# Attention with unnormalised probabilities: the denominators of two heads inverted together and applied to the output by GpSimd

## The chip, the cores and the metric

The kernel runs on one core of a Trainium2 chip. A core has a matrix engine (TensorE, PE in the profile, with its weight loads listed apart as PEld), a vector engine (VectorE, DVE), a scalar engine (ScalarE, ACT), GpSimd (POOL) and SyncE (SP), which issues most of the DMAs. The engines run their own instruction streams in order and wait for each other by semaphores. The metric is the device time of one execution in microseconds, the median of three runs.

## The reference

One layer of a hybrid encoder block over 1024 tokens of width 1024. What matters here is the neighbourhood attention: 16 heads of width 64 over a 16 x 64 grid of tokens, each query looking at a window of 8 x 16 keys, with a learned bias.

```python
s = jnp.einsum("bjhd,bajchd->bhjac", q_i, k_win).astype(jnp.float32) + bias.astype(jnp.float32)[None]
p = jax.nn.softmax(s.reshape(bsz, NA_HEADS, GRID_W, kh * NA_COLS), axis=-1)
p = p.reshape(bsz, NA_HEADS, GRID_W, kh, NA_COLS).astype(v.dtype)
return jnp.einsum("bhjac,bajchd->bjhd", p, v_win)
...
x = x + jnp.concatenate([y_ssm, y_na.astype(y_ssm.dtype)], axis=-1) @ w_out
```

The attention output and the output of a state-space mixer are put side by side and multiplied by `w_out`; a squared-ReLU MLP follows.

## The kernel before

The program is one stream of work written in a tile framework. The framework's scheduler plans the whole program with a simulated timeline and fixes the order of the instructions on each engine; on the chip each engine keeps that order. Products that need more than one pass are made from operands that are split in a high and a low part (`split_from_psum`, `split_na`, `load_w`: ScalarE writes the high part, VectorE or GpSimd the low part), three matmuls for each product.

The stages in order: input projection and state-space mixer, the projections of q, k and v, the attention stage, the end of the output projection, the MLP in two phases. The change lies in the attention stage (lines 773 to 1006).

**The heads.** Eight pairs of heads are worked through (line 983). `load_qkv(p)` loads q, k (high and low part) and v of a pair with SP's DMAs into tiles of two alternating pools; `bias_for(h)` loads the bias of one head (`braw`) and GpSimd adds a mask to it in three instructions (`mb`, L881, two buffers). `attend` then makes one head, `hh` being 0 or 1 in the pair, in eight blocks of 128 queries. A block `b` sees two or three blocks of 128 keys, so its scores are 128 x 256 or 128 x 384. Its steps are:

- two matmuls (L931, L934) write the scores into a PSUM tile `psc` (two buffers);
- VectorE adds the bias and finds the row's negated maximum (L939, with a second small instruction that reads the accumulator); ScalarE takes the exponential and its row sum `db` (L949, again with an accumulator read);
- VectorE inverts the row sum (L957) and multiplies the probabilities by it (L958);
- TensorE transposes the two or three 128 x 128 pieces (L962) into a PSUM tile `ptp` (two buffers, shared with `pty` below), ScalarE and VectorE split them into `pth` and `ptl` (L184, L185);
- `weigh(b - 3)` multiplies the values by the transposed probabilities of an earlier block (L908), and where four blocks of queries are complete ScalarE copies the high half and VectorE adds the low half into `yT` (L918, L919).

`yT` holds a pair's output as 128 rows (two heads of 64) by 1024 tokens in one buffer; after the pair SP stores it to `na_dr[p]` (L996).

**The filler.** Between the blocks the output projection is worked off: `w_out_part(0..2)` is a generator of 48 steps, each one an output tile of 12 matmuls of 128x512 (`po`, L178 to L180) and one VectorE addition (L833). Two steps are made ahead of the attention, then 44 over its 128 blocks (line 973), two behind the last block, and `fill(-1)` makes whatever is left. Parts 0 and 1 read the mixer's output from `y_dr`; part 2 reads `na_dr[0..3]`. Their weights come by `load_w`, which loads 512 KB, lets ScalarE write the high part (L148) and GpSimd the low part (L149).

**The end of the stage.** The fourth part of the output projection takes `na_dr[4..6]`, read back and split by ScalarE and GpSimd while pair 7 is worked on (lines 985 to 991), and the last pair's `yT`, split straight from SBUF by ScalarE (L789) and VectorE (L790). Its matmuls run in the loop at line 1069, with the products of `na_dr[4]`, `[5]`, `[6]` and of pair 7 as `k` = 0, 1, 2, 3 of each tile.

Of the kernel before, what the change touches and what calls it, by code (L numbers as in the profile page):

```python
# [1 line left out]

# [1 line left out]

# [14 lines left out]
P = 128  # L19
# [36 lines left out]
def hymba_block(  # L56
# [66 lines left out]
    y1_dr = dr.tile([NT, P, D], F32, name="y1_dr")  # L123
    y_dr = dr.tile([NT, P, D], F32, name="y_dr")
    na_dr = dr.tile([NT, P, D], F32, name="na_dr")
    cum_dr = dr.tile([2, P, P], F32, name="cum_dr")
    t2_dr = dr.tile([16, 16, 8, 384], F32, name="t2_dr")
    t1_dr = dr.tile([16, 8, 31, 24], F32, name="t1_dr")
# [644 lines left out]
    with ExitStack() as ph:  # L773
# [18 lines left out]
        def w_out_part(part, yt):  # L792
            for f in range(4 * part + len(yt), 4 * part + 4):
                yl = yp.tile([P, T], F32R, tag="yl", name="yl", bufs=4)
                yh = yp.tile([P, T], F32R, tag="yh", name="yh", bufs=4)
                yf = yl.bitcast(F32)
                if f < 8:
                    nc.sync.dma_start(
                        yf.rearrange("p (c f) -> p c f", c=NT),
                        y_dr[:, :, f * P : (f + 1) * P].rearrange("c p f -> p c f"),  # L800
                    )
                    pts = []
                    for h in range(2):
                        pt = ps_tp("pty")
                        for j in range(4):
                            c = 4 * h + j
                            nc.tensor.transpose(
                                pt[:, j * P : (j + 1) * P], yf[:, c * P : (c + 1) * P], ident
                            )
                        pts.append(pt)  # L810
                    for h in range(2):
                        s = slice(h * 512, (h + 1) * 512)
                        split_from_psum(
                            yh[:, s], yl[:, s], pts[h], pcol[:, 72 + f : 73 + f]
                        )
                else:
                    nc.sync.dma_start(yf, na_dr[f - 8])
                    split_na(yh, yl, yf, nc.gpsimd)
                yt.append((yh, yl))
            for h, t in ((h, t) for h in range(2) for t in range(NT)):  # L820
                if t == 0:
                    get = load_w_nat(w_out[0], 512 * part, 4, 512 * h, nc.gpsimd)
                pt = ps_mm("po")
                s = slice(t * P, (t + 1) * P)
                for k in range(4):
                    yh, yl = yt[k]
                    mm3(pt, yh[:, s], yl[:, s], *get(k), k == 0, k == 3)
                d = x2[:, t, h * 512 : (h + 1) * 512]
                if part == 0:
                    nc.sync.dma_start(  # L830
                        d, x[0, t * P : (t + 1) * P, h * 512 : (h + 1) * 512]
                    )
                nc.vector.tensor_tensor(d, d, pt, op=add)  # L833
                yield
# [54 lines left out]
        pth = ap.tile([P, NT, 3, P], F32R, name="pth", bufs=1)  # L889
        ptl = ap.tile([P, NT, 3, P], F32R, name="ptl", bufs=1)  # L890

        def attend(hh, mb, q, k, kl, v, yT):
            hp = slice(HD * hh, HD * hh + HD)
            nmx = ap.tile([P, 8], F32, tag="nmx", name="nmx")
            den = ap.tile([P, 8], F32, tag="den", name="den")
            pv = [ps_v("pv0"), None]

            def weigh(g):
                b0, b1 = max(g - 1, 0), min(g + 2, NT)
                for i in range(2):  # L900
                    c0, c1 = max(b0, 4 * i), min(b1, 4 * i + 4)
                    if c0 >= c1:
                        continue
                    first, last = g == 3 * i, g == 4 + 3 * i
                    if first and i:
                        pv[1] = ps_v("pv1")
                    for pt in (pth, ptl):
                        pvm = nc.tensor.matmul(  # L908
                            pv[i][:, (c0 - 4 * i) * P : (c1 - 4 * i) * P],
                            lhsT=v[:, g, hh],  # L910
                            rhs=pt[:, g, c0 - g + 1 : c1 - g + 1, :],
                            start=first and pt is pth,
                            stop=last and pt is ptl,
                            skip_group_check=True,
                        )
                    if last:
                        yo = to_grid(yT[hp], i)
                        nc.scalar.copy(yo, from_blocks(pv[i][0:HD]))  # L918
                        nc.vector.tensor_tensor(  # L919
                            yo, yo, from_blocks(pv[i][HD:P]), op=add  # L920
                        )
                return pvm

            for b in range(NT):
                g0, g1 = max(b - 1, 0), min(b + 2, NT)
                m = g1 - g0
                n = m * P
                o = (3 if b == 0 else 5 if b == NT - 1 else 0) * P
                qs, ks = slice(b * P, (b + 1) * P), slice(g0 * P, g1 * P)
                pt = ps_s("psc")  # L930
                nc.tensor.matmul(  # L931
                    pt[:, 0:n], lhsT=q[:, hh, qs], rhs=k[:, hh, ks], start=True, stop=False
                )
                mark = nc.tensor.matmul(  # L934
                    pt[:, 0:n], lhsT=q[:, hh, qs], rhs=kl[:, hh, ks], start=False, stop=True
                )
                pr = ap.tile([P, 384], F32, tag="pr", name="pr", bufs=4)
                db = den[:, b : b + 1]
                nc.vector.tensor_tensor_reduce(  # L939
                    pr[:, 0:n],  # L940
                    pt[:, 0:n],
                    mb[:, o : o + n],
                    scale=-1.0,
                    scalar=3.0e38,
                    op0=add,
                    op1=ALU.min,
                    accum_out=nmx[:, b : b + 1],
                )
                nc.scalar.activation(  # L949
                    pr[:, 0:n],  # L950
                    pr[:, 0:n],
                    AF.Exp,
                    bias=nmx[:, b : b + 1],
                    scale=-1.0,
                    accum_out=db,
                )
                nc.vector.reciprocal(db, db)  # L957
                nc.vector.tensor_scalar(pr[:, 0:n], pr[:, 0:n], db, None, op0=mul)  # L958
                pp = ps_tp("ptp")
                for j in range(m):  # L960
                    s = slice(j * P, (j + 1) * P)
                    nc.tensor.transpose(pp[:, s], pr[:, s], ident)  # L962
                s0 = 2 * g0 + b + 1
                hi, lo = (
                    t.rearrange("p g s q -> p (g s) q")[:, s0 : s0 + 2 * m - 1 : 2, :]
                    for t in (pth, ptl)
                )
                pv3 = pp[:, 0:n].rearrange("p (j q) -> p j q", q=P)
                split_from_psum(hi, lo, pv3)
                if b > 2:  # L970
                    weigh(b - 3)
                done[0] += 1
                if done[0] * 44 // 128 > (done[0] - 1) * 44 // 128:
                    with tc.issue_after(mark.ins):
                        fill()
            weigh(NT - 3)
            weigh(NT - 2)
            return mark, weigh(NT - 1)

        filler += [w_out_part(0, []), w_out_part(1, []), w_out_part(2, [])]  # L980
        last = []
        fill(2)
        for p in range(8):
            q, k, kl, v = load_qkv(p)
            if p == 7:
                for j, tag in enumerate(("q", "k", "v")):
                    hl = b0.tile([P, 2, T], F32R, tag=tag, name="hl", bufs=1)
                    yf = hl[:, 1].bitcast(F32)
                    nc.sync.dma_start(yf, na_dr[4 + j])
                    split_na(hl[:, 0], hl[:, 1], yf, nc.gpsimd)  # L990
                    last.append((hl[:, 0], hl[:, 1]))
            yT = yt.tile([P, T], F32, tag="yT", name="yT", bufs=1)
            for hh in range(2):
                marks = attend(hh, bias_for(2 * p + hh), q, k, kl, v, yT)
            if p < 7:
                nc.sync.dma_start(na_dr[p], yT)  # L996
            else:
                hl = b0.tile([P, 2, T], F32R, tag="kl", name="hl", bufs=1)
                split_na(hl[:, 0], hl[:, 1], yT, nc.vector)
                last.append((hl[:, 0], hl[:, 1]))  # L1000
        for i in (0, 1):
            with tc.issue_after(marks[i].ins):
                fill()
# [391 lines left out]
```

## Time and profile before

| | |
|---|---|
| median of three runs | 1681.8 us (1676.36 to 1685.55) |
| the profiled execution: span | 1676.4 us, equal to the fastest of the three runs to 0.1 us |
| its mean granted TensorE clock | 0.986 |
| attention stage, first softmax to last output tile | 674 to 966 us of the span |
| before it: projections and mixer | 0 to 674 us |
| behind it: end of the output projection | 966 to 1025 us |
| MLP | 1025 to 1676 us |

The busy time of TensorE in the profile counts overlapping matmuls once, and the end of each matmul is modelled, so a high busy share does not mean that no more matmuls would fit; the starts of matmuls that follow each other show how fast they are really issued. The list of waits names for each idle time of an engine the instruction that ended it.

### The profile page before, as it was taken

What the parts mean: (1) busy time and instruction counts of PE and PEld (TensorE: products, weight loads), DVE (VectorE), ACT (ScalarE), POOL (GpSimd) and SP (SyncE); (2) the same over time, 40 slices, a digit from 0 to 9 for tenths busy, and PEclk for the clock granted to TensorE, in tenths of its full rate; (3) what the DMA queues carried; (4) which work ended last, traced back from release to release, by engine and by line L of the source; (5) the groups of instructions that cost most, each with busy time, mean ns of one, the idle gap of its engine ahead of it and who ended that gap; (6) DMA issues with size and microseconds to landing.
All of it is one profiled execution on the core that took longest, in us unless ns stands there. A gap on an engine that the chain in (4) does not pass through costs nothing. (4 is left out here: it accounts for less than half of the span.)

```text
span 1676.4 us, 20931 instructions
## 1 busy us (share of the span) xinstructions
PE 1590.8 (95%) x7453; PEld 1297.3 (77%) x7453; DVE 1106.0 (66%) x1686; ACT 721.3 (43%) x1187; POOL 708.4 (42%) x506
## 2 busy tenths in 40 slices
PE   6999999998988899998999989999999989999999
PEld 5788888777766678887778767788888868888887
DVE  5767214788796852888898867544243387887863
ACT  5434223434343442556565533554444444433330
POOL 4000003888687862322243232244444465455551
PEclk9999999999999999999999999999999989999999
DMA  8113337876666785956664141353344386644231
GB/s 217 51 38 105 93 100 212 215 194 196 229 220 173 218 263 190 281 165 185 180 190 118 62 164 50 101 201 126 138 164 150 127 295 231 216 149 151 101 101 75
DMA packets 178755, 269.75 MB, mean 161 GB/s; under 512 B 14219, under 2 KB 105307, under 8 KB 178651
## 3 DMA queue, kind: packets, MB, share of 16 engines
q1 hardware_dynamic: 134667, 227.51, 44.1%
q10 hardware_dynamic: 42976, 37.23, 7.3%
q0 software_dynamic: 1008, 3.67, 0.5%
q8 instruction: 59, 0.97, 0.3%
q14 instruction: 45, 0.37, 0.1%
HBM read 185.21 MB, written 86.50 MB: 162 GB/s over the span
## 5 line engine op out<-in xcount | busy, mean ns | idle before, releaser
L760 POOL TENSOR_TENSOR wl<-wraw,wh 128x1024 fp32r<-128x1024 f32 x110 | 298.5, 2724 | 318.4 <-ACT wh L759 297.1
L759 ACT ACTIVATE wh<-wraw 128x1024 fp32r<-128x1024 f32 x110 | 115.6, 1054 | 149.7 <-PE px L745 50.8
L745 PE MATMUL px<-wh,ahl 128*128 128x512 f32 x512 | 162.5, 395 | 3.3 <-ACT ahl L759 3.3
L179 PE MATMUL pq<-wl,hTh 128*128 128x512 f32 x384 | 153.6, 402 | 4.9 <-DVE wl L149 4.8
L178 PE MATMUL pq<-wh,hTh 128*128 128x512 f32 x384 | 154.4, 405 | 3.5 <-ACT wh L148 3.5
L745 PE MATMUL px<-h,wh 128*128 128x512 f32 x496 | 156.0, 396 | 1.4 <-DVE x L1078 1.4
L180 PE MATMUL pq<-wh,hTl 128*128 128x512 f32 x384 | 152.9, 399 | 0.0
L760 DVE TENSOR_TENSOR ahl<-ar,ahl 128x1024 fp32r<-128x1024 f32 x56 | 115.1, 2062 | 23.2 <-ACT ahl L759 22.1
L759 ACT ACTIVATE ahl<-ar 128x1024 fp32r<-128x1024 f32 x56 | 58.2, 1052 | 140.1 <-PE px L745 75.3
L745 PEld LDWEIGHTS px<-wh,ahl 128*128 128x128 f32 x512 | 97.0, 190 | 25.0 <-ACT ahl L759 3.7
L745 PEld LDWEIGHTS px<-h,wh 128*128 128x128 f32 x496 | 93.2, 188 | 24.0 <-ACT h L184 1.6
L149 DVE TENSOR_TENSOR wl<-wraw,wh 128x1024 fp32r<-128x1024 f32 x40 | 55.3, 1386 | 81.9 <-ACT wh L148 81.2
L745 PE MATMUL px<-wl,ahl 128*128 128x512 f32 x256 | 101.0, 395 | 0.0
L745 PE MATMUL px<-h,wl 128*128 128x512 f32 x248 | 98.1, 395 | 0.0
L881 POOL TENSOR_TENSOR mb<-braw,nam 128x256 f32<-128x256 f32 (+1 forms) x48 | 40.1, 863 | 131.1 <-DVE nmx L939 72.2
L179 PEld LDWEIGHTS pq<-wl,hTh 128*128 128x128 f32 x384 | 73.6, 192 | 23.1 <-DVE wl L149 8.6
L149 POOL TENSOR_TENSOR wl<-wraw,wh 128x1024 fp32r<-128x1024 f32 x18 | 43.0, 2401 | 110.5 <-ACT wh L148 110.5
L178 PEld LDWEIGHTS pq<-wh,hTh 128*128 128x128 f32 x384 | 74.0, 193 | 20.2 <-ACT wh L148 5.2
L184 ACT ACTIVATE pth<-ptp 128x384 fp32r<-128x384 f32 (+1 forms) x128 | 57.7, 455 | 73.1 <-PE ptp L962 72.5
L612 POOL TENSOR_TENSOR rb<-rb,c 128x512 f32<-128x512 f32 x64 | 77.0, 1223 | 20.4 <-DMA rb<-cum_dr 19.2
L180 PEld LDWEIGHTS pq<-wh,hTl 128*128 128x128 f32 x384 | 73.5, 191 | 15.0
L745 PE MATMUL pz<-h,wh 128*128 128x512 f32 x256 | 80.8, 396 | 0.8 <-DVE h L185 0.8
(268 smaller groups left out, 4211.4 us busy)
## 6 DMA issues: line engine op xcount, KB each, us to landing
ar<-act_dr SPq DMA_DIRECT2D x56, 512.0 KB, 3.7
act_dr<-cq SPq DMA_DIRECT2D x49, 512.0 KB, 3.2
wraw<-in_w_in_dram SPq DMA_DIRECT2D x44, 512.0 KB, 4.3
rb<-cum_dr SPq DMA_DIRECT2D x32, 512.0 KB, 7.2
wraw<-in_w_mlp_in_dram SPq DMA_DIRECT2D x32, 512.0 KB, 4.6
wraw<-in_w_mlp_out_dram SPq DMA_DIRECT2D x32, 512.0 KB, 5.2
q_dr<-hl ACTq DMA_DIRECT2D x64, 128.0 KB, 3.6
k_dr<-hl ACTq DMA_DIRECT2D x16, 512.0 KB, 5.3
```

The costliest lines, as they stand in the source:

```text
L149: lo_eng.tensor_tensor(lo[:, 0:n], raw[:, 0:n], hi[:, 0:n].bitcast(F32), op=sub)
L178: nc.tensor.matmul(pt, lhsT=ah, rhs=bh, start=first, stop=False)
L179: nc.tensor.matmul(pt, lhsT=ah, rhs=bl, start=False, stop=False)
L180: return nc.tensor.matmul(pt, lhsT=al, rhs=bh, start=False, stop=last)
L184: nc.scalar.activation(hi, src, AF.Copy)
L612: nc.gpsimd.tensor_tensor(rb[:, d], rb[:, d], c1[:, d, c, h0 : h0 + 4].unsqueeze(2).broadcast_to([P, 4, P]), op=sub,)
L745: nc.tensor.matmul(pt, lhsT=a, rhs=b, start=f, stop=l, skip_group_check=True)
L759: nc.scalar.activation(hl[0], src, AF.Copy)
L760: eng.tensor_tensor(hl[1], src, hl[0].bitcast(F32), op=sub)
L881: nc.gpsimd.tensor_tensor(mb[:, s].rearrange("p (s r c) -> p s r c", r=16, c=8), v[:, a:b], nam[:, s].rearrange("p (s r c) -> p s r c", r= ...
```

## The change

The probabilities are no longer multiplied by the inverted row sum in each block. A tile `den` of 128 x 2 x 8 collects the row sums of both heads of a pair. A new function `divide(p, yT, den)` inverts all 16 columns in one VectorE instruction, transposes them on TensorE to 16 rows of 128, copies these with ScalarE, and SP stores them to DRAM (`rd_dr[p]`). Two SP DMAs read them back, each broadcast to 64 partitions, as a tile `rb` of 128 x 1024; GpSimd multiplies `yT` by it in two instructions. The store of `yT` follows.

For pairs 0 to 6 `divide` is called in the next pair's first head behind block 3; for pair 7 directly behind the last block. The read-back of `na_dr[4..6]` moves into `divide(6)`. `yT` gets two buffers. The filler rate falls from 44 to 40 steps in 128 blocks, so that four more steps are left behind the last block. The scratch memory that the program reserves for GpSimd's DMA descriptors is set to 4096 bytes per partition.

```diff
-        def attend(hh, mb, q, k, kl, v, yT):
+        def attend(hh, mb, q, k, kl, v, yT, den, late):
...
-            den = ap.tile([P, 8], F32, tag="den", name="den")
...
-                db = den[:, b : b + 1]
+                db = den[:, hh, b : b + 1]
...
-                nc.vector.reciprocal(db, db)
-                nc.vector.tensor_scalar(pr[:, 0:n], pr[:, 0:n], db, None, op0=mul)
...
+                if b == 3 and late:
+                    late.pop()()
                 done[0] += 1
-                if done[0] * 44 // 128 > (done[0] - 1) * 44 // 128:
+                if done[0] * 40 // 128 > (done[0] - 1) * 40 // 128:
...
+        def divide(p, yT, den):
+            dv = den.rearrange("p h b -> p (h b)")
+            nc.vector.reciprocal(dv, dv)
+            pt = ps_tp("ptd")
+            nc.tensor.transpose(pt[0:16, 0:P], dv, ident)
+            rd = ap.tile([16, P], F32, tag="rd", name="rd", bufs=1)
+            nc.scalar.copy(rd, pt[0:16, 0:P])
+            nc.sync.dma_start(rd_dr[p], rd)
+            rb = ap.tile([P, T], F32, tag="rb", name="rb", bufs=1)
+            for j in range(2):
+                nc.sync.dma_start(
+                    rb[j * HD : (j + 1) * HD],
+                    rd_dr[p, 8 * j : 8 * j + 8].rearrange("b q -> (b q)").partition_broadcast(HD),
+                )
+            for h in range(2):
+                yo = to_grid(yT, h)
+                nc.gpsimd.tensor_tensor(
+                    yo, yo, from_blocks(rb[:, h * 512 : (h + 1) * 512]), op=mul
+                )
+            if p < 7:
+                nc.sync.dma_start(na_dr[p], yT)
+            else:
+                hl = b0.tile([P, 2, T], F32R, tag="kl", name="hl", bufs=1)
+                split_na(hl[:, 0], hl[:, 1], yT, nc.vector)
+                last.append((hl[:, 0], hl[:, 1]))
+            if p == 6:
                 for j, tag in enumerate(("q", "k", "v")):
...
-            yT = yt.tile([P, T], F32, tag="yT", name="yT", bufs=1)
+            yT = yt.tile([P, T], F32, tag="yT", name="yT", bufs=2)
+            den = ap.tile([P, 2, 8], F32, tag="den", name="den")
             for hh in range(2):
-                marks = attend(hh, bias_for(2 * p + hh), q, k, kl, v, yT)
-            if p < 7:
-                nc.sync.dma_start(na_dr[p], yT)
...
+                marks = attend(hh, bias_for(2 * p + hh), q, k, kl, v, yT, den, late)
+            late.append(partial(divide, p, yT, den))
+        late.pop()()
...
-    nc = bacc.Bacc("TRN2", target_bir_lowering=False, num_devices=1)
+    nc = bacc.Bacc(
+        "TRN2", target_bir_lowering=False, num_devices=1, dynamic_dma_scratch_size=4096
+    )
```

More of the change, by code (lines that the diff above doesn't have):

```diff
@@ L1 @@
 from contextlib import ExitStack
+from functools import partial
 import numpy as np
@@ L125, in hymba_block @@
     na_dr = dr.tile([NT, P, D], F32, name="na_dr")
+    rd_dr = dr.tile([8, 16, P], F32, name="rd_dr")
     cum_dr = dr.tile([2, P, P], F32, name="cum_dr")
@@ L978, in attend @@
             return mark, weigh(NT - 1)
[L980 to L985, printed above, removed]
+        def divide(p, yT, den):
[24 more added lines that the diff above has]
+            if p == 6:
                 for j, tag in enumerate(("q", "k", "v")):
@@ L991, in hymba_block @@
                     last.append((hl[:, 0], hl[:, 1]))
-            yT = yt.tile([P, T], F32, tag="yT", name="yT", bufs=1)
-            for hh in range(2):
-                marks = attend(hh, bias_for(2 * p + hh), q, k, kl, v, yT)
-            if p < 7:
-                nc.sync.dma_start(na_dr[p], yT)
[L997 to L1000, printed above, removed]
+        filler += [w_out_part(0, []), w_out_part(1, []), w_out_part(2, [])]
+        last = []
+        late = []
+        fill(2)
+        for p in range(8):
+            q, k, kl, v = load_qkv(p)
+            yT = yt.tile([P, T], F32, tag="yT", name="yT", bufs=2)
+            den = ap.tile([P, 2, 8], F32, tag="den", name="den")
+            for hh in range(2):
+                marks = attend(hh, bias_for(2 * p + hh), q, k, kl, v, yT, den, late)
+            late.append(partial(divide, p, yT, den))
+        late.pop()()
         for i in (0, 1):
```

## The prediction

> **What bounds the kernel now.** I read three parts of the page first: the busy times, the 40 slices, the chain that ended last. The chain covers only the MLP, so it says nothing of the stage that changes; I then asked for the busy time by stage.
>
> ```profile
> PE 1590.8 (95%) x7453; PEld 1297.3 (77%) x7453; DVE 1106.0 (66%) x1686; ACT 721.3 (43%) x1187; POOL 708.4 (42%) x506
> 674.00:966.00 292.00, 276.64 (x1535) 233.61 (x1534) 252.29 (x732) 175.28 (x446) 80.17 (x62) 0.99 0.58 168
> 1025.00:1676.00 651.00, 636.48 (x2752) 515.81 (x2752) 384.08 (x335) 263.21 (x301) 296.87 (x118) 0.99 0.44 151
> ```
>
> The columns of the two window rows are the window, its length, the busy time and count of PE, PEld, DVE, ACT and POOL, then the granted clock, the DMA share and GB/s. Over the whole program PE looks full. In the attention stage, 674 to 966 us, DVE is busy for 252.3 of 292 us (86%), in the MLP for 59%.
>
> PE's 276.6 us are not a measure of what the stage must take, because matmuls overlap. The starts of matmuls that follow each other are:
>
> ```profile
> 966.49 0.39 PE L180 MATMUL po<-wh,yl 128*128 128x512 f32 x1
> 966.71 0.39 PE L178 MATMUL po<-wh,yh 128*128 128x512 f32 x1
> 966.95 0.39 PE L179 MATMUL po<-wl,yh 128*128 128x512 f32 x1
> 967.17 0.39 PE L180 MATMUL po<-wh,yl 128*128 128x512 f32 x1
> ...
> 958.65 0.49 PE L962 MATMUL ptp<-ident,pr 128*128 128x128 f32 x3
> 839.78 0.27 PE L962 MATMUL ptp<-ident,pr 128*128 128x128 f32 x1
> ...
> L807 PE MATMUL pty<-ident,yl 128*128 128x128 f32 x48 | 7.2, 273 | 0.3 <-issue 0.3
> ```
>
> A 128x512 matmul is issued every 0.23 us (0.68 us over three), 0.45 ns per column. Three transposes take 0.49 us from first start to last end and a single one 0.27, so each further one costs 0.11 us. So PE's need in the stage is: filler, 47 steps (the additions of L833 that fall in the window, quoted below) of 12 matmuls, 564 x 0.23 = 130 us; scores, by the code 16 heads with six blocks of 384 and two of 256 columns, twice, 90,112 columns = 40.5 us; values, the same number of columns, 40.5 us; 352 transposes of probabilities (three in 96 blocks, two in 32) and 48 of the mixer's output, 44 us. Together 255 of 292 us, 87%. For the MLP the same count gives 2752 x 0.23 = 633 of 651 us, 97%. The attention stage thus loses 37 us.
>
> Two rows with the columns "us in total, times, longest us" and the idle column of the page's groups say to whom:
>
> ```profile
> PE psc L931 <- DVE nmx L939: 8.9, 8, 2.7
> PE ptp L962 <- DVE den L957: 2.4, 2, 1.9
> PE pv L908 <- ACT pth L184: 1.3, 3, 0.6
> PE ptp L962 <- DVE ptl L185: 1.0, 2, 0.6
> PE pv L908 <- DVE ptl L185: 0.6, 1, 0.6
> ...
> DVE x L833 <- PE po L180: 20.2, 25, 2.1
> ACT pth L184 <- PE ptp L962: 72.5, 50, 4.7
> ```
>
> Of PE's 15.4 us without a matmul (292 - 276.6), 14.2 are waits for the softmax's chain, nearly all for DVE. DVE in its turn waits 20.2 us for filler matmuls: both queues are in order, both need some 2 us of the 2.28 us that a block takes (292/128), and neither can run ahead of the other for long. Neither bounds the stage alone; their alternation does. Two of the long waits are followed by a lower clock:
>
> ```profile
> 760.00:780.00 20.00, 16.10 (x93) 13.21 (x92) 18.98 (x52) 13.75 (x35) 9.04 (x8) 0.91 0.95 277
> 780.00:800.00 20.00, 19.92 (x110) 16.60 (x109) 16.08 (x45) 10.89 (x27) 0.00 (x0) 1.00 0.34 82
> 860.00:880.00 20.00, 16.94 (x92) 14.29 (x90) 18.42 (x45) 15.24 (x33) 12.49 (x8) 0.91 0.78 270
> ```
>
> At 0.91 instead of 1.00 each such slice of 20 us loses 1.8 us, 3.6 us together. The remaining 37 - 14.2 - 3.6 = 19 us are small losses at each change between kinds of matmul.
>
> **The change, part by part.** What leaves VectorE:
>
> ```profile
> L958 DVE TENSOR_SCALAR pr<-pr,den 128x384 f32<-128x384 f32 x96 | 45.6, 481 | 1.2
> L833 DVE TENSOR_TENSOR x<-x,po 128x512 f32<-128x512 f32 x47 | 32.1, 684 | 20.4 <-PE po L180 20.2
> L958 DVE TENSOR_SCALAR pr<-pr,den 128x256 f32<-128x256 f32 x32 | 23.3, 729 | 0.4
> L957 DVE RECIPROCAL den<-den 128x1 f32<-128x1 f32 x128 | 19.4, 155 | 0.3
> ```
>
> 45.6 + 23.3 + 19.4 = 88.3 us of DVE go. The 256-wide multiply is slower on average than the 384-wide one, so some of these are held up by something beside them; that goes too. In each block's chain the step from exponential to transposes becomes shorter by 0.155 + about 0.5 us. Eight inversions of 16 columns come back, at 0.16 to 0.4 us each (between the 128x1 row and a 128x256 row of L185 or L939) under 3.2 us; I take 1.6. DVE then needs 166 us, 61% of a stage of 274 us, as in the MLP. What is late next is ACT, at 175 us, and PE itself.
>
> **The gain** is put together from the 37 us. Of the 14.2 us of waits I let 11 go: the chain still passes DVE, ACT, PE, ACT and DVE with two buffers in PSUM, so some stay. The clock's 3.6 us go. Of the 19 us of small losses I let 4 go, a fifth, since they hang on weight loads as well (bounds 0 and 19). That is 18.6 us.
>
> **What is added on PE:** eight transposes at 0.11 us, 0.9 us, each holding one of the two `ptp` tiles until ScalarE's copy of 16 rows, bounded by 0.19 us (accumulator read) and 0.58 us (L918). Eight of these, under 4.6 us on an ACT with over 100 us idle: nothing.
>
> **What is added on GpSimd and the queues.** The nearest rows:
>
> ```profile
> L612 POOL TENSOR_TENSOR rb<-rb,c 128x512 f32<-128x512 f32 x64 | 77.0, 1223 | 20.4 <-DMA rb<-cum_dr 19.2
> L149 POOL TENSOR_TENSOR wl<-wraw,wh 128x1024 fp32r<-128x1024 f32 x11 | 26.3, 2409 | 54.2 <-ACT wh L148 54.2
> POOL mb L881 <- DVE nmx L939: 72.2, 7, 15.5
> na_dr<-yT SPq DMA_DIRECT2D x7, 512.0 KB, 5.9
> kl<-k_dr SPq DMA_DIRECT2D x14, 256.0 KB, 10.2
> braw<-t_dr SPq DMA_DIRECT2D x13, 192.0 KB, 5.0
> ```
>
> Sixteen multiplies of 128x512 at 1.22 us are 19.6 us, on a POOL that is busy 80 of 292 us: beside other work. On the way are a store of 8 KB and two broadcast loads of 256 KB. For the store I take 3 us (bounds 0 and the 5.9 of 512 KB); for the loads together 7 us (5.0 for 192 KB, 10.2 for two halves of 64 partitions like these, in a busy stage). SP waits for ScalarE's copy, then for the store to land; behind it stand loads of `braw`, `x` and weights. In pairs 0 to 6 nobody needs `yT` soon: `na_dr[p]` is read two pairs later or in pair 7, and the second `yT` buffer lets the next pair write. So these cost nothing while GpSimd's own later work is not held (the slower rival).
>
> [...]
>
> **The end of the stage** is where the new chain is exposed, since the last pair's `divide` feeds the output projection at once.
>
> ```profile
> 960.07 0.50 ACT L949 ACTIVATE pr<-pr,nmx 128x256 f32<-128x256 f32 x1
> 960.47 0.19 ACT L949 ACTIVATION_READ_ACCUMULATOR pr<-pr,nmx 128x1 f32 x1
> ...
> 964.53 0.27 PE L908 MATMUL pv<-ptl,v 128*128 128x256 f32 x1
> 967.24 1.04 ACT L789 ACTIVATE hl<-yT 128x1024 fp32r<-128x1024 f32 x1
> 968.32 2.56 DVE L790 TENSOR_TENSOR hl<-yT,hl 128x1024 fp32r<-128x1024 f32 x1
> 970.43 0.40 PE L178 MATMUL po<-wh,hl 128*128 128x512 f32 x1
> ```
>
> Call 960.7 us, when the last row sum is there, E. The new chain: inversion, transpose and copy 1.2 us, store 3, loads 7, two multiplies 2.4, ScalarE's split 1.04, VectorE's 2.56: E + 17.2 us (by the bounds E + 12 to E + 23). Against it stands PE's work. The last value matmul ends 4.1 us behind E; then one filler step is left today (964.64 to 967.40 us, 12 x 0.23), with the change five, 13.8 us; the first matmul that needs the last pair follows 3.0 us later (970.43 against 967.40). That is E + 20.9 us. So the four steps hide the chain by 3.7 us; at the far bound 2.4 us stick out. They add no work, being taken from the 44. Cost: 0. The read-back of `na_dr[4..6]` moves 9 us later into pair 7, with three ScalarE splits and three of 2.4 us on GpSimd, and has the rest of that pair, over 25 us: 0.
>
> ```profile
> L1179 POOL DMA_DIRECT2D act_dr<-cq x7: 531/531/767, 1328.6 to 1359.0; - x7
> ```
>
> A smaller memory for GpSimd's DMA descriptors touches these seven stores alone, 5 us apart on average in the MLP: 0, at most their own 7 x 0.5 us once more.
>
> **Sum:** -18.6 + 0.9 = -17.7 us on the profiled execution, 1676.4 us (its span equals the time of the fastest run), so 1658.7 us. That execution lies 5.4 us under the median of the three; against the median of 1681.8 it is 1664 us, 1.05% less. A difference of over 0.5%, 8.4 us, is about what a measurement of this kernel can tell from none; the three runs spread over 9 us.
>
> **Rivals.**
>
> *Hidden anyway.* PE is the bound and VectorE's time was beside it. For it: PE is 95% busy and only 15.4 us of the stage are idle. Then half of the 14.2 us go, -7 + 0.9 = -6 us: 1676 us. Against it: the count of starts, 255 of 292 us, and the waits by name.
>
> [...]
>
> *Full relief.* With DVE at the MLP's share the stage reaches the MLP's 97%: 255/0.97 = 263 us, -29 + 0.9 = -28 us: 1654 us. For it: the same DVE share in both. Against: the MLP has no chain from PE through three engines and back.
>
> *Slower: GpSimd stands still in front of its multiply.* Its queue is in order. The multiply waits from the issue of the store to the landing of the loads, 3 + 7, at the bounds up to 16 us, in each pair. If the planned order puts a weight split (L149) behind it, the filler matmuls on PE wait for the low part. Twelve weight pieces fall on eight pairs; six stalls of which PE feels 6 us each are 36 us, against the gain +18 us: 1700 us. It decides from 3 us per stall (the gain is gone) and 4.4 us (slower by 0.5%). For it: 10 us are longer than any lead that I can read off for L149. Against: POOL is idle in 73% of the stage (80.17 of 292 us busy), waits 54.2 us for ScalarE in front of L149, and `mb` is made one head, some 18 us, ahead.
>
> *It doesn't do what it says:* the scheduler plans all anew and may set the freed time against a worse order elsewhere. Nothing in the trace bounds this; I let it widen the range by a few us.
>
> **Chances.** Forecast (-9 to -24 us) 0.53; full relief 0.14; hidden (-8 to +8) 0.24; slower 0.09. So faster by over 0.5% 0.67, within 0.23 (a little of the hidden case falls outside), slower 0.10. The range leaves out the slower case and the tail of full relief: 1647 to 1686 us.
>
> **What will show it.** In the changed kernel's stage DVE should fall to about 166 us, PE's waits for L939 to a few us, and the stage from 292 to about 274 us while its last four filler steps stand behind the last value matmul. The loads of `rb` should land within 10 us of the copy. A wait of `po` on POOL's `wl`, or of POOL on DMA `rb` with PE idle beside it, shows the slower rival; a gap of PE at the first use of the last pair shows the tail. I am wrong if PE keeps its waits although DVE is idle: then PSUM's two buffers, not DVE's load, make them.

## The result and the profile after

The kernel after takes 1677.6 us (median of 20 runs, 1673.2 to 1682.4) against 1681.8 us for the kernel before (20 runs, 1676.2 to 1686.5): ratio 0.9974, 95% interval 0.9962 to 0.9986. Measured once more, beside other runs (e0), the ratio was 0.9989 (0.9972 to 1.0007). The gain is some 2 to 4 us; the prediction had 17.7 us and forecast 1664 us. The time lies inside the range given (1647 to 1686), but the gain lies below the 9 to 24 us of the forecast: a change within 0.5% had been given a chance of 0.23.

To compare runs I measure the stage from the first softmax (L939, after: L940) to the first matmul of the last part of the output projection (its products of `na_dr[4]`; those of the last pair follow about 3 us later). One row of busy time by window is shown for the kernel before and one for the kernel after, and a third for what follows in the kernel after, up to the first matmul of the MLP. The columns are those of the window rows above: length, then busy time and count of PE, PEld, DVE, ACT and POOL, the granted clock, DMA share, GB/s.

```profile
674.00:967.40 293.40, 278.04 (x1541) 234.73 (x1540) 252.43 (x732) 176.41 (x448) 80.17 (x62) 0.99 0.58 168
```

```profile
679.00:971.00 292.00, 282.08 (x1550) 235.66 (x1549) 184.73 (x485) 177.02 (x457) 98.48 (x79) 0.99 0.65 184
971.00:1028.70 57.70, 52.24 (x242) 41.86 (x240) 40.38 (x48) 21.19 (x34) 22.44 (x20) 0.97 0.39 137
```

DVE lost 67.7 us of its 252.4, POOL took 18.3 us more, and the stage became 1.4 us shorter. It begins 5 us later in the profile of the kernel after; the order of the instructions before the stage is the same but for two neighbours on ScalarE, and the start moved between 671.5 and 679.0 us over the runs below, so this is put down to chance and lengths are compared instead of ends. What speaks for chance: the start lies at 676.5 to 679.0 us in the five profiled executions that were slower than their kernel's median (after, e0, e2, e4, e5), and at 671.5 to 674.0 us in the four that were faster (before, e1, e6, e7). The two profiled executions also lie on opposite sides of their medians, which is why their whole times say nothing of the change: the spans are 1676.4 us before and 1680.6 us after, and where both are on record a run's time is 1.8 to 2.1 us longer than its span. So the profile before is of a run of about 1678.2 us, not of the fastest of the three, and the one after is of the slowest, 1682.4 us.

Three views of the kernel after, in its stage, answer to the rows of the prediction: the waits (engine, line, waited for: us in total, times, longest), the groups of instructions, and the DMA issues (KB each, median us to landing).

```profile
PE pv L909 <- ACT pth L186: 3.2, 3, 2.7
PE psc L932 <- DVE nmx L940: 3.1, 8, 0.6
...
PEld psc L932 <- DVE nmx L940: 11.3, 37, 0.8
...
POOL yT L997 <- DMA rb<-rd_dr: 31.3, 6, 8.4
...
ACT hl L791 <- DMA hl<-na_dr: 7.2, 2, 5.2
```

```profile
L835 DVE TENSOR_TENSOR x<-x,po 128x512 f32<-128x512 f32 x47 | 32.0, 685 | 69.4 <-PE po L182 69.3
...
L997 POOL TENSOR_TENSOR yT<-yT,rb 128x512 f32<-128x512 f32 x16 | 20.3, 1293 | 50.2 <-DMA rb<-rd_dr 31.3 <-DVE x L835 10.6 <-issue 8.4
```

```profile
rb<-rd_dr SPq DMA_DIRECT2D x16, 256.0 KB, 4.6
...
hl<-na_dr SPq DMA_DIRECT2D x3, 512.0 KB, 4.1
rd_dr<-rd SPq DMA_DIRECT2D x8, 8.0 KB, 2.8
```

A row of SP's own waits, up to 960 us, belongs to the last of these: how long the loads of `rb` wait for the store in front of them.

```profile
SPq L991 <- DMA rd_dr<-rd: 17.7, 8, 5.7
```

The wait that the change was meant against shrank: PE's matmuls wait 3.1 us for L940 instead of 8.9, none longer than 0.6 us. But PE now waits 3.2 us for ScalarE's `pth`, nearly all of it once (2.7 us), and DVE waits 69.3 us for filler matmuls where it waited 20.2: what left DVE became idle time of DVE.

The one long wait can be followed in the timeline (start, length, engine, line; in brackets how long the engine sat idle before, and what ended it):

```profile
903.92 2.53 POOL L997 TENSOR_TENSOR yT<-yT,rb 128x512 f32<-128x512 f32 x2 [7.15 <-DMA rb<-rd_dr]
...
906.47 0.33 SPq L1001 DMA_DIRECT2D na_dr<-yT  x1
...
909.14 0.79 SPq L1010 DMA_DIRECT2D hl<-na_dr  x2
...
910.99 0.28 PE L935 MATMUL psc<-kl,q 128*128 128x256 f32 x1
912.47 1.06 ACT L791 ACTIVATE hl<-hl 128x1024 fp32r<-128x1024 f32 x1 [5.20 <-DMA hl<-na_dr]
913.43 0.85 ACT L186 ACTIVATE pth<-ptp 128x384 fp32r<-128x384 f32 x2
...
913.95 0.69 PE L909 MATMUL pv<-pth,v 128*128 128x384 f32 x1 [2.68 <-ACT pth L186]
```

```profile
880.00:900.00 20.00, 19.44 (x114) 16.51 (x114) 14.16 (x39) 16.37 (x42) 16.36 (x11) 1.00 0.87 288
900.00:920.00 20.00, 16.50 (x78) 14.29 (x77) 9.56 (x25) 9.37 (x24) 8.93 (x7) 0.83 0.36 116
920.00:940.00 20.00, 19.84 (x110) 16.33 (x109) 12.17 (x34) 13.02 (x34) 5.26 (x4) 1.00 0.16 49
```

GpSimd scales pair 5's output only at 903.9 us, when `rb` has landed (the longest wait for a store of denominators, 5.7 us, lies in front of these loads, which leave at 898.7 us); its store leaves at 906.5; the read-back of that same tensor can leave at 909.1 and lands 3.3 us later. ScalarE's split of it (L791) was planned earlier and stands at the head of ScalarE's queue for 5.2 us. Behind it stands `pth`, and for that PE stands still for 2.7 us. Then the clock falls: 0.83 over a slice of 20 us is 3.4 us lost. Together 6.1 us, over half of the 10.5 us that the stage gains in the run without the division, below.

The end of the stage:

```profile
951.93 0.19 ACT L950 ACTIVATION_READ_ACCUMULATOR pr<-pr,nmx 128x1 f32 x1
952.80 0.24 DVE L983 RECIPROCAL den<-den 128x16 f32<-128x16 f32 x1
...
955.47 0.27 PE L985 MATMUL ptd<-ident,den 128*16 128x128 f32 x1
...
955.77 0.25 ACT L987 COPY rd<-ptd 16x128 f32<-16x128 f32 x1 [1.30 <-PE ptd L985]
...
956.05 0.32 SPq L988 DMA_DIRECT2D rd_dr<-rd  x1
...
957.41 1.09 SPq L991 DMA_DIRECT2D rb<-rd_dr  x2
...
962.58 2.54 POOL L997 TENSOR_TENSOR yT<-yT,rb 128x512 f32<-128x512 f32 x2 [10.58 <-DVE x L835]
...
965.15 1.06 ACT L791 ACTIVATE hl<-yT 128x1024 fp32r<-128x1024 f32 x1 [8.39 <-POOL yT L997]
...
966.25 1.23 DVE L792 TENSOR_TENSOR hl<-yT,hl 128x1024 fp32r<-128x1024 f32 x1 [3.88 <-ACT hl L791]
...
967.39 1.28 DVE L835 TENSOR_TENSOR x<-x,po 128x512 f32<-128x512 f32 x2
...
968.12 0.51 PE L180 MATMUL po<-wh,yh 128*128 128x512 f32 x1 [0.99 <-DVE x L835]
...
973.97 0.40 PE L180 MATMUL po<-wh,hl 128*128 128x512 f32 x1
```

The last row sum is there at 952.1 us; the chain ends at 967.5, 15.4 us later. PE has other work until 974.0 us, where the first product of the last pair stands (the filler until 971.0, then the products of the other pairs). So the chain is hidden. What PE loses here, 1.0 us, is something else: VectorE's half of the last split waits 3.9 us in VectorE's queue for ScalarE, and two additions of the filler, ready before it, stand behind it.

### The profile page after: what moved, and what is told of

Same layout as the page of the kernel before. It is cut to its first block, busy times and chain, and to the rows that moved or that the text cites. A ratio compares the mean times of both kernels' runs of the same rounds, so it can differ in the third digit from the quotient of the medians.

```text
span 1680.6 us, 20886 instructions
## 1 busy us (share of the span) xinstructions
PE 1596.8 (95%) x7461; PEld 1301.1 (77%) x7461; DVE 1031.1 (61%) x1438; ACT 722.1 (43%) x1195; POOL 727.7 (43%) x522
## 5 line engine op out<-in xcount | busy, mean ns | idle before, releaser
L762 POOL TENSOR_TENSOR wl<-wraw,wh 128x1024 fp32r<-128x1024 f32 x110 | 299.7, 2736 | 317.6 <-ACT wh L761 303.1
L761 ACT ACTIVATE wh<-wraw 128x1024 fp32r<-128x1024 f32 x110 | 115.6, 1054 | 151.2 <-PE px L747 51.2
L181 PEld LDWEIGHTS pq<-wl,hTh 128*128 128x128 f32 x384 | 74.0, 193 | 20.9 <-DVE wl L151 6.2
L150 ACT ACTIVATE wh<-wraw 128x1024 fp32r<-128x1024 f32 x58 | 61.1, 1056 | 46.3 <-PE px L181 19.2
L747 PE MATMUL pz<-wh,ahl 128*128 128x512 f32 x256 | 80.5, 390 | 0.0
```

Of the source, the lines that this page charges most:

```text
L150: nc.scalar.activation(hi[:, 0:n], raw[:, 0:n], AF.Copy)
L181: nc.tensor.matmul(pt, lhsT=ah, rhs=bl, start=False, stop=False)
L747: nc.tensor.matmul(pt, lhsT=a, rhs=b, start=f, stop=l, skip_group_check=True)
L761: nc.scalar.activation(hl[0], src, AF.Copy)
L762: eng.tensor_tensor(hl[1], src, hl[0].bitcast(F32), op=sub)
```

## The experiments

"Stage" is measured as above; "removal alone" is the kernel before without the division, whose output is therefore not normalised.

| | median, us | ratio to before (95%) | stage, us |
|---|---|---|---|
| before | 1681.8 | | 293.4 |
| after | 1677.6 | 0.9974 (0.9962 to 0.9986) | 292.0 |
| e0, after again | 1677.4 | 0.9989 (0.9972 to 1.0007) | 292.2 |
| e1, removal alone | 1668.6 | 0.9924 (0.9897 to 0.9951) | 282.9 |
| e2, pair 6 from SBUF | 1678.3 | 0.9981 (0.9965 to 0.9998) | 293.1 |
| e3, TensorE alone | 1663.5 (1 run) | | 265.2 |
| e4, rate 44 | 1679.0 | 0.9990 (0.9973 to 1.0007) | 286.0 |
| e5, split ordered later | 1675.2 | 0.9968 (0.9952 to 0.9984) | 286.7 |
| e6, load beside the chain | 1686.3 | 1.0023 (1.0003 to 1.0042) | 295.7 |
| e7, e5 and the last split on GpSimd | 1673.6 | 0.9957 (0.9940 to 0.9974) | 285.4 |
| e8, no low half | 1656.6 (1 run) | | 268.1 |
| e9, transposes of a constant | 1699.9 (1 run) | | 313.3 |
| e10, low half unread | 1687.4 (1 run) | | 298.3 |

The outputs of e3, e6 and e8 to e10 are not those of the layer either. The kernel before had medians of 1680.3 us beside e0 to e3 and 1681.0 us beside e4 to e7; beside e8 and e9 it took 1681.0 us and beside e10 1674.2 us, one run each. In each experiment the scheduler plans the order anew, so an edit can move more than what it names.

### e0 and e1: the change again, and its removal without its additions

e1 is the kernel before without two lines:

```diff
-                nc.vector.reciprocal(db, db)
-                nc.vector.tensor_scalar(pr[:, 0:n], pr[:, 0:n], db, None, op0=mul)
```

> The changed kernel once more, to see how far one profiled execution differs from another. Stage here means: from the first softmax instruction on VectorE to the first matmul of the last part of the output projection (before 674.1 to 967.4 us = 293.3 us; after 679.0 to 971.0 us = 292.0 us). If the start of the stage, 679 against 674 us, is chance of the execution, it comes out elsewhere within some 5 us while the stage's length stays at 292 +- 1 us; if the change moved the start (other addresses, other waits), it is again at 679. Ratio to before 0.997.

> The kernel before without the inversion and the multiplication in each block; nothing in their place, so the probabilities stay unnormalised and the output is not scaled. Theory 1 (TensorE itself needs some 275 us for this stage, since its short matmuls expose their weight loads, so freed VectorE time can only buy a part of the 19 us of long gaps): stage 284 to 288 us, ratio 0.994 to 0.997. Theory 2 (the removal is worth what was forecast, and what was added took it back): stage 274 to 277 us, ratio 0.989 to 0.991. VectorE's busy time in the stage falls by 88 us in both.

The window row of e1's stage, then three of its waits:

```profile
671.50:954.40 282.90, 275.62 (x1542) 233.92 (x1541) 185.09 (x476) 175.21 (x448) 78.05 (x62) 0.99 0.63 175
```

```profile
DVE x L833 <- PE po L180: 58.7, 37, 3.0
...
PEld psc L931 <- DVE nmx L939: 8.2, 22, 1.1
...
PE psc L931 <- DVE nmx L939: 3.3, 6, 0.8
```

Removing the division buys 10.5 us in the stage (293.4 to 282.9), 12 us in the medians. The kernel after has the same DVE load (184.7 against 185.1 us) and is 9.1 us slower in the stage. The 282.9 us lie between the 274 to 277 and the 284 to 288 us of the two theories. Two questions follow: what takes the 9.1 us back, and why the removal buys 10.5 us and not 18.6.

### e2, e5, e7: the read-back and the last split

e2 is the kernel after in which pair 6 is split straight from SBUF, like pair 7, and the read-back of pairs 4 and 5 is called directly behind `load_qkv(7)`:

```diff
-            if p < 7:
+            if p < 6:
                 nc.sync.dma_start(na_dr[p], yT)
...
-                split_na(hl[:, 0], hl[:, 1], yT, nc.vector)
+                split_na(hl[:, 0], hl[:, 1], yT, {6: nc.gpsimd, 7: nc.vector}[p])
...
+            if p == 7:
+                read_back()
```

> The changed kernel with another read-back for the last part of the output projection: na_dr[4] and [5] are loaded and split at the start of pair 7, as before the change, and pair 6's output is split straight from SBUF without the way through DRAM. Theory 3 (the moved read-back costs: ScalarE stands still for 5.2 us in front of the split that waits for the load, TensorE stands 2.8 us at 911 us and then runs at half clock for 6.8 us, 3.4 us): both gone, stage 286 us instead of 292, ratio to before 0.993 to 0.994. Rival (the gap was only one of the stage's chance gaps and others take its place): stage 290 to 292 us, ratio 0.996 to 0.998.

```profile
ACT hl L791 <- DMA hl<-na_dr: 5.8, 1, 5.8
PE pv L909 <- ACT pth L186: 3.7, 3, 3.2
```

These two waits of e2 show that nothing was cured: ScalarE still stood 5.8 us for the read-back of pair 5, whose store is as late as before, and PE 3.2 us for `pth`. What decides is not who is read back but where ScalarE's instruction stands relative to the store. So e5 leaves all transfers as they are in the kernel after and only has each split issued behind the latest exponential:

```diff
-                nc.scalar.activation(
+                ex[0] = nc.scalar.activation(
...
-                    split_na(hl[:, 0], hl[:, 1], yf, nc.gpsimd)
+                    with tc.issue_after(ex[0].ins):
+                        split_na(hl[:, 0], hl[:, 1], yf, nc.gpsimd)
```

e7 is e5 with the low half of pair 7 made by GpSimd, so that nothing waits in VectorE's queue:

```diff
-                split_na(hl[:, 0], hl[:, 1], yT, nc.vector)
+                split_na(hl[:, 0], hl[:, 1], yT, nc.gpsimd)
```

> The changed kernel, where ScalarE's splits of the read-back tiles na_dr[4..6] are queued behind the exponential of block 3 of pair 7's first head, instead of where the planner puts them (in pair 6, in front of a load that has not landed). Theory 3 (the planned place costs 2.9 us of TensorE's waiting and 3.4 us of half clock behind it, because the store of pair 5 is late by the way of its denominators through DRAM): the gap at 911 us and the lower clock behind it go, stage 285 to 287 us, ratio 0.993 to 0.995. Rival (another wait takes its place): 290 to 292 us, ratio 0.997 to 0.999.

> e5 and besides the low half of the last pair's split on GpSimd instead of VectorE, so that VectorE does not stand in front of it with two additions of the filler behind it (TensorE's gap of 1.1 us at 967 us in the trace after). If both losses are what the trace after shows: stage 284 to 286 us, ratio 0.993 to 0.994, near e1. If the order that the planner makes anew brings other gaps: 288 to 292 us, ratio 0.996 to 0.999.

For e5 the same slice of 20 us and the wait for the read-back; for e7 the end of the stage:

```profile
900.00:920.00 20.00, 19.54 (x111) 16.63 (x110) 12.61 (x35) 11.88 (x30) 6.19 (x6) 1.00 0.27 90
```

```profile
ACT hl L791 <- DMA hl<-na_dr: 2.3, 1, 2.3
```

```profile
953.05 0.69 DVE L835 TENSOR_TENSOR x<-x,po 128x512 f32<-128x512 f32 x1 [2.06 <-PE po L182]
...
954.62 2.41 POOL L792 TENSOR_TENSOR hl<-yT,hl 128x1024 fp32r<-128x1024 f32 x1 [1.17 <-ACT hl L791]
955.80 0.69 DVE L835 TENSOR_TENSOR x<-x,po 128x512 f32<-128x512 f32 x1 [2.06 <-PE po L182]
```

In e5 PE is busy 19.5 of the 20 us at full clock where the kernel after had 16.5 at 0.83, and the stage is 5.3 us shorter. In e7 VectorE's additions run as their tiles are done; 1.3 us more. That is 6.6 of the 9.1 us, and eight transposes (0.9 us) were forecast; some 1.6 us are not assigned. Both stages came out as expected (285 to 287 and 284 to 286 us). e7 is the fastest of the complete kernels, 0.9957 of the kernel before. The intervals of e7 and of the kernel after overlap; the two stages are told apart by the waits that are gone, not by the medians.

### e4: without the cover at the end

The kernel after with the old filler rate, 44 steps in 128 blocks instead of 40.

```diff
-                if done[0] * 40 // 128 > (done[0] - 1) * 40 // 128:
+                if done[0] * 44 // 128 > (done[0] - 1) * 44 // 128:
```

> The changed kernel with the filler rate of before, 44 steps in 128 blocks, so that the four steps behind the last block are gone. If the tail's cover is worth what the forecast said (the chain of the last pair ends 15.4 us behind the last row sum in the trace after, and without the four steps TensorE's work ends some 10 us behind it), TensorE stands some 5 us in front of the last pair's first product: stage 296 to 298 us, ratio to before 1.000 to 1.002. Rival (the four steps do nothing, something else hides the chain or the order is made anew): stage 291 to 293 us, ratio 0.997 to 0.999.

```profile
PE po L180 <- ACT hl L791: 5.8, 1, 5.8
```

PE reaches the last part of the output projection 6.0 us sooner (286.0 us) and, where the last pair's products begin, waits 5.8 us for the last split. So the wait lies behind the stage as it is measured here, and the 296 to 298 us that were expected of it can't show: behind the stage 64.9 us pass until the MLP instead of 57.7, and stage and rest together are 350.9 us against 349.7. The four steps hide the chain, as the forecast counted on. What they are worth in all is not shown, because the planned order is another one: in e4 ScalarE waits at most 2.3 us at a time for the read-back, the slice from 900 to 920 us is granted 1.00 (the stage as a whole 0.99). The medians of e4 and of the kernel after, 1.4 us apart, don't tell the two from each other.

### e3, e6, e8, e9, e10: what the removal is worth

e3 leaves out softmax, division, splits and the copies into `yT`; its operands are constants, so only PE's own work of the stage is left. e6 is removal alone plus the same two instructions on VectorE, beside the chain:

```diff
+                dm = ap.tile([P, 385], F32, tag="dm", name="dm", bufs=1)
+                nc.vector.reciprocal(dm[:, 384:385], db)
+                nc.vector.tensor_scalar(dm[:, 0:n], pr[:, 0:n], 2.0, None, op0=mul)
```

> TensorE's own need: the kernel before, where the attention's matmuls and transposes are all issued but read constant tiles (transposes from the mask, values with constant probabilities); softmax, splits of probabilities and output evacuation are left out, the filler is whole. Nothing of the attention waits for VectorE or ScalarE. From the first value or transpose matmul of the attention to the last part of the output projection: by the forecast's count 255 us (0.45 ns per column, 0.11 us per transpose); by theory 1 270 to 277 us, with the same 0.08 us more at each short matmul that the trace after shows (128x384 scores 0.258 instead of 0.175 us).

> The kernel of e1 (no inversion, no multiplication in the chain, output not scaled) with the same two VectorE instructions added beside the chain: each block's inversion and multiplication write a tile that nobody reads. VectorE's busy time in the stage is again some 250 us, but the step from exponential to transposes is short. If VectorE's load made the loss of before: stage 291 to 294 us, ratio to before 0.998 to 1.001. If the length of the chain made it: stage 282 to 285 us, ratio 0.991 to 0.994.

A window row of e3 and its one slice of lower clock, then a window row of e6 with PE's longest wait:

```profile
679.30:944.50 265.20, 261.48 (x1536) 233.01 (x1535) 43.21 (x62) 29.27 (x33) 72.00 (x50) 0.99 0.60 171
...
760.00:780.00 20.00, 16.28 (x98) 15.23 (x98) 2.23 (x4) 3.49 (x4) 9.39 (x8) 0.91 0.80 215
```

```profile
673.90:969.60 295.70, 279.20 (x1541) 234.80 (x1541) 243.34 (x732) 177.33 (x448) 80.25 (x63) 0.99 0.57 167
```

```profile
PE psc L931 <- DVE nmx L939: 11.4, 13, 2.0
```

PE's own need is, as an estimate from these rows, about 260 us: e3's 265.2, less one stop of 3.7 us for a load (265.20 - 261.48), less the 1.8 us that the clock lost in the slice of that stop (0.91 over 20 us), plus some 2 us because 18 score matmuls lay ahead of this window and only 4 ahead of the stage in the kernel before, less the 2.1 us by which the first filler matmul comes before the first softmax there. That is 2 us less than the expectations of e8 and e9 reckon with. It lies between the 255 us of the forecast's count and the 270 to 277 us of theory 1. So the kernel before loses some 33 us in the stage, not 37.

In e6 the path from the exponential to the transposes is as short as in e1, and the loss is back (295.7 us; 291 to 294 had been expected for this case): it comes from the two instructions on VectorE, not from their being a link between exponential and transposes. PE waits 11.4 us for L939 again. Whether it is the time that they take or their place in VectorE's in-order queue, e6 doesn't separate. (e6 and e10 also have the 4096 bytes of descriptor memory of the kernel after. The seven DMAs that GpSimd issues itself lie behind the stage, from 1328.6 us in the kernel before and from 1333.2 us in the kernel after, and take 531 ns, median, in both.)

Of the 33 us, e1 leaves 23. The last three runs ask what those are. All are e1 with one more edit: in e8 the low part of the transposed probabilities is a constant zero tile and VectorE's subtraction (L185) is left out; in e9 the transposes read a constant tile instead of the probabilities; e10 is e8 with the subtraction made into a spare tile that nobody reads.

```diff
-                split_from_psum(hi, lo, pv3)
+                nc.scalar.activation(hi, pv3, AF.Copy)
```

```diff
-                    nc.tensor.transpose(pp[:, s], pr[:, s], ident)
+                    nc.tensor.transpose(pp[:, s], ident, ident)
```

```diff
+                sp = ap.tile([P, 3, P], F32R, tag="sp", name="sp", bufs=1)
+                nc.vector.tensor_tensor(sp[:, 0:m], pv3, hi.bitcast(F32), op=ALU.subtract)
```

> The kernel before without the inversion and the normalising multiply, and also without VectorE's low part of the transposed probabilities: the low part is a constant zero tile, so the three value matmuls are all still made, with one factor zero. VectorE loses a further 65 us of its 185 us in the stage, and the step from the transposes to the value matmuls loses VectorE. The stage with VectorE's load reduced by the two normalising instructions alone took 282.8 us, TensorE alone took 265.2 us with a 3.9 us gap of a load among them, so some 20 us are open. If they are VectorE's load, most of the proportion seen so far holds (68 us of load removed bought 10.5 us): the stage falls by 8 to 12 us to 271 to 275 us. If they come from the chain through the score buffers (VectorE's L939 with 0.4 to 0.6 us between scores and the release of their buffer) and from matmuls that start on a fresh wait, the stage stays within 3 us of 282.8.

> The kernel before without the inversion and the normalising multiply, in which the transposes read a constant tile instead of the probabilities: the softmax is still made, with all of VectorE's and ScalarE's work, but TensorE waits for it only where a score buffer has to come free. VectorE's load is that of the removal alone, 185 us. If the 20 us between that kernel (282.8 us) and TensorE alone (262 us without its load gap) come from VectorE's load and the score buffers, the stage stays at 279 to 283 us. If they come from the chain from the scores through the exponential to the transposes, it falls to 268 to 274 us.

> The kernel before without the inversion and the normalising multiply, in which the low part of the transposed probabilities is a constant zero tile for the value matmuls, as in e8_no_low_half; VectorE still makes the subtraction of the low part, into a spare tile that nobody reads. VectorE's load is again that of the removal alone (about 185 us in the stage), while no value matmul waits for it; its hold on the transposes' buffers is back. Without the subtraction the stage took 268.1 us, with the subtraction on the path 282.8 us. If VectorE's load makes the difference, the stage is 279 to 284 us. If the step in the chain from the transposes to the value matmuls makes it, the stage stays at 267 to 272 us.

The window row of e8's stage; then e10's, with two of its waits:

```profile
674.80:942.90 268.10, 264.70 (x1542) 232.03 (x1541) 126.51 (x348) 175.40 (x448) 80.74 (x63) 1.00 0.63 184
```

```profile
675.60:973.90 298.30, 283.14 (x1541) 235.98 (x1540) 184.98 (x476) 175.82 (x448) 80.72 (x63) 0.99 0.56 166
```

```profile
PEld pv L909 <- ACT pth L968: 14.5, 31, 1.0
...
PE pv L909 <- ACT pth L968: 7.1, 19, 0.7
```

In e8 the stage falls by a further 14.8 us, more than the 8 to 12 us expected, to within some 8 us of PE alone, with the same matmuls. Its second 59 us of VectorE (185.1 to 126.5) buy more than the first 67 did. In e10 no value matmul waits for VectorE, its busy time is e1's again, and the stage is slower than before the change, outside both ranges that were expected. So taking L185 off the way to the value matmuls is not enough to make e8 fast, and the zero operand isn't either, since e10 has it too. How much of e10's 298.3 us is the load itself is open: the planned order is another one, in which value matmuls wait for ScalarE's `pth` 19 times, 7.1 us in all, and their weight loads 14.5 us, where e8 has 0.7 and 2.3 us. So VectorE's load alone doesn't fix the length of the stage: e1 and e10 have the same busy time of VectorE and are 15.4 us apart.

e9 told nothing. Without the wait for the probabilities the scheduler ran scores ahead, the value matmuls ended 56 us behind the last softmax, `mb` waited 60.6 us for `braw`, and the clock was 0.95. It is neither of the two numbers that were expected.

## Why the prediction was wrong

Three rows of VectorE's timeline in the kernel before bear on the first point (start, length):

```profile
840.16 0.53 DVE L185 TENSOR_TENSOR ptl<-ptp,pth 128x384 fp32r<-128x384 f32 x1
840.62 0.34 DVE L958 TENSOR_SCALAR pr<-pr,den 128x256 f32<-128x256 f32 x1
840.88 0.54 DVE L939 CUSTOM_DVE_ANT_0 pr<-psc,mb 128x384 f32<-128x384 f32 x1
```

- **What leaves VectorE: over-sized.** The step counted 88.3 us off and 166 us left. 67 us left and 185 stayed, in e1 already. The 88.3 us are a sum of durations, but each instruction's record begins before the one ahead of it ends (840.62 against 840.16 + 0.53), by some 0.08 us. VectorE's groups in the stage add up to 294.5 us of durations where the window row has 252.4 us of busy time, so a group's sum is more than what its removal frees.
- **The gain of 18.6 us: over-sized. This step failed, and it is the largest miss.** It let 11 of 14.2 us of waits, 3.6 us of clock and 4 of 19 us of small losses go. e1, which has just the removal, got 10.5 us. The count of PE's need (255 us) was some 5 us low, so the loss was some 33 us and not 37; and a third of it went, where the step let half go. The direction of the argument holds: e6 puts the two instructions back and the loss with them, e8 takes more load away and three quarters of the loss go. But e10 shows that the planned order can cost as much as the load.
- **The read-back of `na_dr[4..6]` moves, "and has the rest of that pair, over 25 us: 0".** This step failed too. It asked how long the data has, and not where the splits stand in ScalarE's in-order queue and which store they wait for. Scaling makes pair 5's store late, the split waits for it in front of `pth`, and PE pays 2.7 us and the clock 3.4 us. e5 moves only the split: 5.3 us come back.
- **GpSimd and the queues at 0, apart from that: right in the stage.** `yT` waits for `rb` 31.3 us in all and up to 8.4 us, as the slower rival had it, but PE showed no wait for GpSimd's weight splits. The rival's mechanism, a multiply that waits for its loads, did bite, through the store behind it instead of through L149.
- **The multiplies, the store and the loads:** 1.29 us instead of 1.22; 4.6 us each (median) instead of 7 for both, 5.2 us from the first issue to the multiply at the end of the stage. For the store one number doesn't fit: the row gives a median of 2.8 us where 3 was taken, but the loads behind it left 1.4 us after its issue at the end of the stage (956.05 to 957.41) and 6.1 us after it for pair 5 (892.62 to 898.74), the pair on which the read-back waits.
- **The end of the stage: right, by terms that were off both ways.** The chain took 15.4 us where E + 17.2 was worked out. Inversion, transpose and copy took 3.9 us, not 1.2, since the transpose starts only at 955.5 us, among the last value matmuls; the store took 1.4 us, not 3, the loads 5.2, not 7, and VectorE's half 1.23, not 2.56. The cover reached to 21.9 us behind E (974.0 us; 20.9 forecast), and e4 shows that without the four steps PE stands 5.8 us. Not seen was the 1.0 us by which VectorE's split holds two additions; e7 shows it.
- **"Hidden anyway", 1676 us, came nearest in time, for another reason.** It said that half of the waits would go because PE is the bound. PE isn't: with the same matmuls the stage takes 268 us in e8, less than the 278 us that PE is busy in the kernel before. So there was room.
- **"I am wrong if PE keeps its waits although DVE is idle."** That happened in part: PE's matmuls without work fell from 15.4 to 9.9 us, but weight loads for new scores still wait 11.3 us for L940 (13.6 for L939 before), while VectorE stands 69.3 us for filler matmuls. Whether the score buffers or the alternation of two in-order queues make the remaining losses of e1 isn't settled; e10 could not separate it.

For the stage the forecast was 17.7 us, and 1.4 came. Of the 16.3 us between them 8.1 are the over-sized gain (18.6 against the 10.5 of e1), 5.3 the read-back (e5), 1.3 the last split (e7), and 1.6 are not assigned.

The stage explains 1.4 of the 4.1 us between the medians. The rest may lie in the stage's own spread, since there is one profile of the kernel before; this stays open.

## What to carry to other kernels

When a step makes a tensor's last write later, follow the store that carries it and every read-back of it to the instruction that consumes it, and look what stands behind that instruction on its engine: an in-order queue with a planned early reader turns a late store into a stall of something unrelated (here 5.2 us of ScalarE, and by it 2.7 us of PE). Order the reader behind work that is due anyway, as e5 does. And before removing load, measure the removal alone, without what the change puts in its place: it gives what there is to gain, here 10.5 us, and leaves the additions to be counted against it.

## What the runs showed of the hardware

- The clock fell after short stops, and the loss doesn't follow from their length alone. In the kernel after PE stood 2.7 us, with 0.5 us more just before, and lost 3.4 us to the clock (0.83 over 20 us). In the kernel before, the longest wait for L939, 2.7 us too, lies in a slice that lost 1.8 us (0.91, 760 to 780 us), and the longest for L957, 1.9 us, in another that lost as much (0.91, 860 to 880 us). In e2 PE stood 3.2 us for `pth`, and the slice from 900 to 920 us was granted 0.83 as in the kernel after.
- Two loads of `rb`, 256 KB each into 64 partitions, issued one behind the other from 957.4 us, had both landed by 962.6 us, 5.2 us later, where the median of one is 4.6 us. Neither the 7 us nor the 10.2 us that the prediction weighed for the pair was needed.
- The way of 8 KB of denominators through DRAM is mostly waiting, and the wait varies: SP waited 17.7 us in eight times for the store to land, once 5.7 us, beside 0.25 us for ScalarE's copy and 0.24 us for inverting 16 columns.
